# The seven-product output projection: weight sums by accumulating DMA, sums of y on VectorE with other signs, first product added to x2 from PSUM

## The chip, the cores and the metric

The kernel runs on one NeuronCore of a Trainium2 chip. The metric is device time in microseconds (us) of one execution. TensorE (PE in the profile, its weight loads PEld) multiplies, VectorE (DVE), ScalarE (ACT) and GpSimd (POOL) do the elementwise work, and SyncE (SP) issues nearly all transfers. Each engine takes its own instructions in order and waits on semaphores. [...]

## The reference, cut to what matters

One decoder block on 1024 tokens of width 1024, all in float32:

```
h  = RMSNorm(x)
p  = h @ w_in          -> q, k, v of two attentions, gate_swa, gate_mla
A  = sliding-window attention, B = latent attention
y  = sigmoid(gate_swa) * (A @ w_o_swa) + sigmoid(gate_mla) * (B @ w_o_mla)
x2 = x + y @ w_out                                  # the stage that is changed
out = RMSNorm(x2 + SwiGLU(RMSNorm(x2)))
```

## The kernel before

**Arithmetic.** A float32 product is made of three matmuls on numbers that are split into a high part (ScalarE, line 160, rounds it) and a low part (VectorE, line 161, subtracts). So every operand of a matmul costs one ScalarE pass and one VectorE pass. The tiles of the high and low parts of y are named yh and yl, those of w_out woh and wol.

**Seven products.** `y @ w_out` is done by Strassen's method in Winograd's form: y and w_out are cut into four blocks each, and seven block products, numbered 1, 2, 6, 7, 5, 4, 3 in the order in which they run (`X_ORDER`), replace eight. Three of them take sums of blocks of y, and four take sums of blocks of w_out. Each product has four row tiles t, each of 12 matmuls into one PSUM bank (tile xo). Products 1, 2, 5 and 3 use one set of four banks ("A"), products 6, 7 and 4 the other ("B"). Product 2 is added onto product 1 in the same banks, 7 onto 6, 4 onto 7, and 3 onto 5.

**Mixing steps.** Ahead of it, twelve steps (`steps`, a4, b0, b4, a5, ...) make the eight row strips of y. A step "a" multiplies by w_o_swa, a step "b" by w_o_mla. `mix_b` lets GpSimd multiply a strip by its gate (line 1304), then VectorE does a multiply from PSUM (line 1309) and an add (line 1310), and `y_split` makes the first high and low parts. After strips 4 to 7, `y_sums` makes four sums of y blocks on GpSimd, into two tiles ys and back into y. Between the steps `W_LOAD` and `W_WORK` load the four blocks of w_out (tiles wo), split two of them and make four sums of two halves each on GpSimd (`w_sum`; one goes to a tile wt).

**The product loop.** For each product and row tile it runs the 12 matmuls and then `xo_done`: product 1 is copied to SBUF by ScalarE (line 1570, tile xp), all others are added to the residual rows x2 by VectorE (line 175, `x<-xo,x`), and the copy of product 1 is added to x2 by GpSimd, twelve adds (`x<-xp,x`). A list `prep` of 30 splits for products 6, 7, 5, 4 and 3 is worked off between the row tiles, at a rate of 1.9 per tile from product 2 on. At (5, 3) GpSimd makes the first sums of the feed-forward weights (`ffn.mix(0)`, six passes, tiles sm and wr).

**Into the feed-forward network.** From product 4 on, each finished row block of x2 goes through `row_sum` (ScalarE square and sum, line 1583; GpSimd rstd, lines 295 and 298), `row_norm` (VectorE, line 1588, tile xn) and `to_h`, which transposes it on TensorE (line 1422, tile tp) and splits it. `next_h` calls `to_h`, first after product 4's tile t = 2. `Seven.run` runs one product of the feed-forward network; its first product is copied out of PSUM by ScalarE (line 793, tile pu).

**What sets the order.** From product 4 on, the order on TensorE, VectorE, ScalarE and GpSimd is that of the program text. Ahead of that a scheduler places the instructions, and buffers of two pools (21 small and 17 large) decide when a load can start. There, too, each engine runs strictly in the order that came out.

Of the kernel before, what the change touches and what calls it, by code (L numbers as in the profile page):

```python
# [12 lines left out]
ALU = mybir.AluOpType  # L13
# [76 lines left out]
def hybrid_block_kernel(  # L90
# [603 lines left out]
    class Seven:  # L694
# [623 lines left out]
    def y_split(q, k):  # L1318

        if k == 0:  # L1320
            yl[q] = (V("yh", F32R), V("yl", F32R))
        hi, lo = yl[q]
        src = {1: lambda: y[k][:, half(1)], 2: lambda: y[4 + k][:, half(1)], 6: lambda: y[k][:, half(0)],
               7: lambda: y_new[1][:, k], 5: lambda: y_new[0][:, k], 4: lambda: y[4 + k][:, half(0)],
               3: lambda: y[k][:, half(1)]}[q]()
        split(hi[:, k], lo[:, k], src)
        if q == 4:
            y.pop(4 + k)
        if q == 3:
            y.pop(k)  # L1330

    def y_sums(k):

        if k == 0:
            y_new.extend([V("ys") for _ in range(2)])
        s1, s3 = y_new[0][:, k], y_new[1][:, k]
# [6 lines left out]
    wr, wl, t1s = {}, {}, {}  # L1343

    def w_load(i, d):
        wr[(i, d)] = V("wo")
        nc.sync.dma_start(wr[(i, d)], w_out[i, d])

    def w_split(q, j):
# [4 lines left out]
        key = {1: (0, 0), 2: (1, 0), 6: (0, 0), 7: (0, 1), 5: None, 4: (1, 0), 3: (1, 1)}[q]  # L1354
        hi, lo = wl[q]
        split(hi[:, k], lo[:, k], t1s[j] if q == 5 else wr[key][:, k])

    def w_sum(n, j):
        k = slice(2 * j, 2 * j + 2)
        if n == 1:  # L1360
            t1s[j] = U("wt", F32, (P, 2, 512))
        b11, b12, b21, b22 = (wr.get((i, d)) for i in range(2) for d in range(2))
        b11, b12, b21, b22 = (None if w is None else w[:, k] for w in (b11, b12, b21, b22))
        sub(*{1: (t1s[j], b12, b11), 3: (b12, b22, b12), 2: (b11, b22, t1s[j]), 4: (b21, b21, b11)}[n], nc.gpsimd)
# [25 lines left out]
    split_ob(3, 1)  # L1390
    for k, (what, dc) in enumerate(steps):
# [11 lines left out]
        if k in W_LOAD:  # L1403
            w_load(*W_LOAD[k])
        for f, q in W_WORK.get(k, ()):
            for j in range(2):
                f(q, j)
# [3 lines left out]
    x2 = {}  # L1411
# [3 lines left out]
    def to_h(xn, b):  # L1415

        c = b % 4
        pss = []
        for kh in range(2):
# [3 lines left out]
            pss.append(ps)  # L1423
        if b < 4:
# [13 lines left out]
        t23 = U("t23", F32, (P, 2, 4, P))  # L1438
        sub(r[:, 0], pss[0], r[:, 0], nc.vector)
        nc.scalar.copy(t23[:, 1], pss[0])  # L1440
# [118 lines left out]
    p1o = V("xp1")  # L1559
# [4 lines left out]
    def residual(b, d, src, eng):  # L1564
        add(x2[b][:, half(d)], src, x2[b][:, half(d)], eng)
# [307 lines left out]
```

## Time and profile before

| what | value |
|---|---|
| median of 3 runs | 1367.27 us (1367.10 to 1368.41) |
| the profiled execution | 1367.46 us, of which 1365.7 us is the span of the trace |
| TensorE busy in the span | 1331.8 us (98%), 6552 matmuls |
| VectorE, ScalarE, GpSimd busy | 954.9 us, 652.0 us, 657.6 us |
| mean granted clock of TensorE | 0.996 of full speed |
| the product loop | 628.7 to 718.5 us from the span's start |

The profile's tables give, for a group or a single instruction, its start, its duration, and in brackets how long its engine sat idle before it and what released it. A busy time of TensorE counts matmuls that overlap, so what counts for the time are the stretches in which it is idle or in which its granted clock is below 1.

### The profile page before, as it was taken

The page shows a single profiled execution, that of the slowest core. Times are in us where ns is not written, and L with a number is a line of the kernel's source. Part 1 is how long each engine was busy: PE and PEld are TensorE (multiplying, and loading weights), DVE is VectorE, ACT ScalarE, POOL GpSimd, SP SyncE. Part 2 cuts the span into 40 slices and gives each one's busy share as a digit, 9 for nine tenths or more (in the row PEclk, how much of TensorE's full clock was granted, in tenths as well). Part 3 has the DMA queues.
Part 4 walks back from the last instruction along what each step waited for, and adds up shares of the span by engine and source line. Part 5 has one row for each costly group of instructions (what it writes and reads, how often), then busy time and mean ns, then how long its engine had stood idle before and what let it go on. Part 6 is the DMA issues. An engine that isn't in the chain of part 4 may idle for free. (4 is left out here: it accounts for less than half of the span.)

```text
span 1365.7 us, 18965 instructions
## 1 busy us (share of the span) xinstructions
PE 1331.8 (98%) x6552; PEld 1112.6 (81%) x6552; DVE 954.9 (70%) x1499; ACT 652.0 (48%) x1317; POOL 657.6 (48%) x664
## 2 busy tenths in 40 slices
PE   9999999999999999999989899999999999999997
PEld 6899878878788888887867688888888888888886
DVE  7868767676777886579978966666656655664862
ACT  7434766675567776633447323223322322644453
POOL 1115645552166554177644875766655651022421
PEclk9999999999999999999999999999999999999999
DMA  9454322335100110655041344554344415996504
GB/s 365 153 187 158 122 87 81 112 117 181 51 1 13 43 47 17 259 188 185 31 154 50 136 160 156 224 193 162 143 158 162 173 74 184 376 383 250 170 8 147
DMA packets 76945, 200.16 MB, mean 147 GB/s; under 512 B 8625, under 2 KB 15281, under 8 KB 76337
## 3 DMA queue, kind: packets, MB, share of 16 engines
q1 hardware_dynamic: 76704, 198.94, 41.0%
q8 instruction: 52, 0.85, 0.3%
q14 instruction: 45, 0.36, 0.1%
q10 hardware_dynamic: 144, 0.00, 0.0%
HBM read 139.14 MB, written 59.77 MB: 146 GB/s over the span
## 5 line engine op out<-in xcount | busy, mean ns | idle before, releaser
L161 DVE TENSOR_TENSOR wl<-wr,wl 128x512 fp32r<-128x512 f32 x150 | 156.4, 1064 | 76.6 <-ACT wl L160 76.3
L161 DVE TENSOR_TENSOR lrv<-lr,lrv 128x1024 fp32r<-128x1024 f32 x77 | 104.9, 1396 | 50.9 <-ACT lrv L160 47.2
L160 ACT CAST lrv<-lr 128x1024 fp32r<-128x1024 f32 x77 | 80.1, 1052 | 96.7 <-PE fd L169 55.7
L167 PE MATMUL fd<-lrv 128*128 128x512 f32 x308 | 119.8, 389 | 0.0
L168 PE MATMUL fd<-lrv 128*128 128x512 f32 x308 | 119.8, 389 | 0.0
L169 PE MATMUL fd<-lrv 128*128 128x512 f32 x308 | 119.8, 389 | 0.0
L172 POOL TENSOR_TENSOR wr<-wr,sm 128x512 f32<-128x512 f32 (+1 forms) x38 | 46.9, 1244 | 117.7 <-DVE wl L161 111.6
L160 ACT CAST wl<-wr 128x512 fp32r<-128x512 f32 x150 | 87.2, 622 | 3.3 <-DVE wr L816 2.7
L161 DVE TENSOR_TENSOR wl<-sm,wl 128x512 fp32r<-128x512 f32 x60 | 53.4, 915 | 45.5 <-ACT wl L160 45.5
L1146 POOL TENSOR_TENSOR denb<-denb,neg_one 128x1 f32<-128x1 f32 x64 | 36.5, 571 | 74.9 <-ACT p L1145 64.3
L167 PEld LDWEIGHTS fd<-lrv 128*128 128x128 f32 x308 | 57.8, 188 | 12.1
L168 PEld LDWEIGHTS fd<-lrv 128*128 128x128 f32 x308 | 57.8, 188 | 12.0
L169 PEld LDWEIGHTS fd<-lrv 128*128 128x128 f32 x308 | 57.8, 188 | 11.9
L1145 ACT ACTIVATE p<-scb,nmb 128x384 f32<-128x384 f32 (+3 forms) x64 | 47.6, 744 | 36.7 <-DVE nmb L1144 35.0
L161 DVE TENSOR_TENSOR ptl<-pTb,pth 128x512 fp32r<-128x512 f32 (+2 forms) x96 | 50.0, 549 | 13.7 <-ACT pth L160 12.8
L1144 DVE CUSTOM_DVE_ANT_0 scb<-scb,mask 128x384 f32<-128x384 f32 (+3 forms) x64 | 48.5, 757 | 14.0 <-PE scb L1136 13.7
L1478 ACT ACTIVATE act<-sm 128x512 f32<-128x512 f32 x11 | 7.0, 633 | 103.7 <-DVE sm L175 103.7
L295 POOL TENSOR_SCALAR ms<-ss 128x1 f32<-128x1 f32 x32 | 8.6, 270 | 98.6 <-ACT x L397 37.7
L1147 POOL TENSOR_SCALAR p<-p,denb 128x384 f32<-128x384 f32 (+3 forms) x64 | 49.3, 770 | 6.3
L175 POOL TENSOR_TENSOR du<-du,xq 128x512 f32<-128x512 f32 x8 | 16.3, 2054 | 69.5 <-DMA lr<-in_w_down_dram 50.4
L1478 ACT ACTIVATE act<-pu 128x512 f32<-128x512 f32 x22 | 13.9, 632 | 74.7 <-DVE pu L175 74.7
L160 ACT CAST pth<-pTb 128x512 fp32r<-128x512 f32 (+2 forms) x96 | 43.0, 482 | 13.5 <-PE pTb L1161 13.1
(355 smaller groups left out, 4475.1 us busy)
## 6 DMA issues: line engine op xcount, KB each, us to landing
lr<-la_d SPq DMA_DIRECT2D x77, 256.0 KB, 5.4
wr<-in_w_gate_dram SPq DMA_DIRECT2D x22, 512.0 KB, 4.3
wr<-in_w_up_dram SPq DMA_DIRECT2D x22, 512.0 KB, 5.0
wd<-in_w_down_dram SPq DMA_DIRECT2D x22, 512.0 KB, 6.7
rb_d<-wd SPq DMA_DIRECT2D x22, 512.0 KB, 2.6
la_d<-sd SPq DMA_DIRECT2D x22, 512.0 KB, 5.2
lr<-rb_d SPq DMA_DIRECT2D x44, 256.0 KB, 5.4
lr<-in_w_down_dram SPq DMA_DIRECT2D x33, 256.0 KB, 5.5
```

The source lines that it names most:

```text
L160: nc.scalar.copy(hi, src)
L161: (eng or nc.vector).tensor_tensor(lo, src, hi.bitcast(F32), op=ALU.subtract)
L167: nc.tensor.matmul(ps, ah, bh, start=first and i == 0, stop=False, skip_group_check=go_on)
L168: nc.tensor.matmul(ps, ah, bl, start=False, stop=False, skip_group_check=go_on)
L169: nc.tensor.matmul(ps, al, bh, start=False, stop=last and i == n - 1, skip_group_check=go_on)
L172: eng.tensor_tensor(out, a, b, op=ALU.subtract)
L175: eng.tensor_tensor(out, a, b, op=ALU.add)
L1144: nc.vector.tensor_tensor_reduce(s_, s_, m_, 1.0, -NEG, op0=ALU.add, op1=ALU.min, accum_out=nm)
L1145: nc.scalar.activation(p_, s_, AF.Exp, scale=-1.0, bias=nm, accum_out=den)
L1146: nc.gpsimd.tensor_tensor(den, den, neg_one[:, 0:1], op=ALU.pow)
L1147: nc.gpsimd.tensor_scalar(p[:, 0:w], p[:, 0:w], den, 0.0, op0=ALU.mult, op1=ALU.add)
L1478: nc.scalar.activation(dst, src, AF.Silu)
```

## The change

**Weights.** `w_sum` is gone. Each sum of w_out blocks is now made by a DMA that adds its source to what stands in its destination (`w_acc`, issued by GpSimd, in two halves). Blocks are loaded as before through SP; the block (0, 0) is loaded twice, once as the start of the sum t1. Where a difference is needed, ScalarE turns the sign of a block in place first (`w_neg`). Two of the operands come out with the wrong sign, and their split turns it: ScalarE casts with scale -1, VectorE uses one `scalar_tensor_tensor` (lines 1363 and 1364 of the changed kernel) in place of the subtract. The loads and sums start at step 1, where before the first load was at step 4.

**y.** The four sums are formed on VectorE, with signs turned so that one of the two ys tiles falls away.

**First product.** It is no longer copied by ScalarE. VectorE adds or subtracts it from its PSUM bank to three halves of x2 for each t, twelve adds in place of four copies and GpSimd's twelve adds. All eight x2 loads come earlier in the program, at steps 10 and 11.

**Order.** The prep list starts in product 1. `ffn.mix(0)` is cut in two and stands behind the second and fourth `row_sum`. `next_h` can run a product between the transposes and the work on them, which is used once, and the copy `t23[:, 1]` stands ahead of the subtract.

```diff
-        def mix(self, j, eng=None):
+        def mix(self, j, eng=None, m=None):
-            if (j, self.ms[0]) in self.sums:
-                return
-            for m in self.ms:
+            for m in self.ms if m is None else (m,):
+                if (j, m) in self.sums:
+                    continue
...
     def y_sums(k):
-            y_new.extend([V("ys") for _ in range(2)])
+            y_new.append(V("ys"))
...
-        add(s1, a21, a22, nc.gpsimd)
-        sub(s3, a11, a21, nc.gpsimd)
-        sub(a21, s1, a11, nc.gpsimd)
-        sub(a11, a12, a21, nc.gpsimd)
+        add(s1, a21, a22, nc.vector)
+        add(a21, a11, a21, nc.vector)
+        add(a11, s1, a11, nc.vector)
+        add(a12, a11, a12, nc.vector)
...
+    def w_neg(name):
+        for j in range(2):
+            w = wr[name][:, 2 * j:2 * j + 2]
+            nc.scalar.activation(w, w, AF.Copy, scale=-1.0)
+
+    def w_acc(name, src):
+        for j in range(2):
+            k = slice(2 * j, 2 * j + 2)
+            src_ = wr[src][:, k] if isinstance(src, str) else w_out[src[0], src[1]][:, k]
+            nc.gpsimd.dma_start(wr[name][:, k], src_, accum_op=ALU.add)
...
-    W_LOAD = {4: (0, 0), 5: (0, 1), 6: (1, 1), 8: (1, 0)}
-    W_WORK = {7: [(w_split, 1)], 9: [(w_sum, 1)], 10: [(w_sum, 3)], 11: [(w_split, 2), (w_sum, 2)]}
+    W_WORK = {1: [(w_load, "b12", 0, 1)], 2: [(w_load, "t1", 0, 0)], 3: [(w_neg, "b12"), (w_acc, "t1", "b12")],
+              4: [(w_load, "b11", 0, 0)], 5: [(w_acc, "b12", (1, 1))], 6: [(w_split, 1, 0)],
+              7: [(w_split, 1, 1), (w_load, "b21", 1, 0)], 8: [(w_acc, "b11", "b12")], 9: [(w_split, 2, 0)],
+              10: [(w_split, 2, 1)], 11: [(w_neg, "b21"), (w_acc, "b21", "b11")]}
...
     def xo_done(q, t):
-        if q == 1:
-            nc.scalar.copy(p1o[:, t], ps)
-        else:
-            residual(*{2: (4 + t, 0), 6: (4 + t, 1), 7: (t, 1), 5: (t, 1), 4: (t, 0), 3: (4 + t, 1)}[q], ps, nc.vector)
-        if q in (6, 7):
-            residual({6: 4, 7: 0}[q] + t, 1, p1o[:, t], nc.gpsimd)
-        if q == 7:
-            residual(t, 0, p1o[:, t], nc.gpsimd)
+        for b, d, sign in {1: ((t, 0, 0), (t, 1, 0), (4 + t, 1, 1)), 2: ((4 + t, 0, 1),), 6: ((4 + t, 1, 0),), 7: ((t, 1, 1),),
+                           5: ((t, 1, 0),), 4: ((t, 0, 1),), 3: ((4 + t, 1, 1),)}[q]:
+            x_ = x2[b][:, half(d)]
+            (add if sign else sub)(x_, x_, ps, nc.vector)
...
+            if (q, t) == (6, 0):
+                w_load("b22", 1, 1)
-            if (q, t) == (5, 3):
-                ffn.mix(0)
-            n_x += q != 1
-            while prep and 30 - len(prep) < 1.9 * n_x:
+            n_x += 0.4 if q == 1 else 1.8
+            while prep and 30 - len(prep) < n_x:
+                if r + t in (1, 3):
+                    ffn.mix(0, None, "gu"[r + t == 3])
...
-    next_h()
-    ffn.run()
+    next_h(ffn.run)
```

The order that comes out moves rows at these places. Names carry the buffer's number.

**GpSimd between step b1 and the product loop.** Before, with the last gate products (L1304) among sums of y (ys, sg) and of w_out (wt, wo):

```order
L1304 TENSOR_TENSOR sg_6713<-ar_6364,sg_6713 128x1024
L172 TENSOR_TENSOR ys_6632<-sg_6590 128x512
L175 TENSOR_TENSOR ys_6631<-sg_6590,sg_6552 128x512
L172 TENSOR_TENSOR sg_6590<-ys_6631,sg_6590 128x512
L172 TENSOR_TENSOR sg_6590<-sg_6552,sg_6590 128x512
L1304 TENSOR_TENSOR sg_6842<-ar_6448,sg_6842 128x1024
L172 TENSOR_TENSOR wt_6923<-wo_6760,wo_6711 128x1024
L172 TENSOR_TENSOR wt_6925<-wo_6760,wo_6711 128x1024
L172 TENSOR_TENSOR wo_6760<-wo_6798,wo_6760 128x1024 x2
```

Now, from the gate product of step b1 to the first rstd (ms, rstd):

```order
L1304 TENSOR_TENSOR sg_6592<-ar_6195,sg_6592 128x1024
L1352 DMA wo_6638<-wo_6590 128x1024 x2
L1352 DMA wo_6590<-in_w_out_dram 128x1024 x2
L1304 TENSOR_TENSOR sg_6720<-ar_6364,sg_6720 128x1024
L1304 TENSOR_TENSOR sg_6849<-ar_6448,sg_6849 128x1024
L1352 DMA wo_6718<-wo_6590 128x1024 x2
L1352 DMA wo_6847<-wo_6718 128x1024 x2
L295 TENSOR_SCALAR ms_7416<-ss_7414 128x1
L298 TENSOR_TENSOR rstd_7418<-ms_7416,neg_half 128x1
```

GpSimd has no elementwise pass left between the last gate product and the first rstd; four pairs of accumulating DMAs stand there, two pairs of them ahead of the gate product of step b2.

**GpSimd at the rstd of the first four row blocks.** Behind the second rstd now stand three passes of the feed-forward sums, and then the third rstd:

```order
L295 TENSOR_SCALAR ms_7439<-ss_7437 128x1
L298 TENSOR_TENSOR rstd_7441<-ms_7439,neg_half 128x1
L175 TENSOR_TENSOR sm_7445<-wr_7324,wr_7349 128x512
L172 TENSOR_TENSOR sm_7445<-sm_7445,wr_7324 128x512
L172 TENSOR_TENSOR wr_7324<-wr_7324 128x4x128
L295 TENSOR_SCALAR ms_7468<-ss_7466 128x1
L298 TENSOR_TENSOR rstd_7470<-ms_7468,neg_half 128x1
```

Before, the six passes stood ahead of the first rstd, and the eight rstd followed each other with one pass between the last two.

**ScalarE after the third transposed block of the second half.** Before, the copy of the transposed block (t) and its cast stood ahead of the copy of a finished product (pu):

```order
L1440 COPY t_1454_7805<-tp_7795 128x512
L1442 CAST t2h_7677<-t_1454_7805 128x4x128
L793 COPY pu_7824<-fa_7811 128x512
L1448 CAST b22h_7675<-tp_7800 128x4x128
L1449 CAST t3h_7679<-t_1454_7805 128x4x128
```

Now the copy of the product stands first:

```order
L793 COPY pu_7816<-fa_7803 128x512
L1446 COPY t_1453_7818<-tp_7793 128x512
L1449 CAST t2h_7675<-t_1453_7818 128x4x128
L1455 CAST b22h_7673<-tp_7798 128x4x128
L1456 CAST t3h_7677<-t_1453_7818 128x4x128
```

TensorE's own order is the same in both kernels.

More of the change, by code (lines that the diff above doesn't have):

```diff
@@ L1402, in hybrid_block_kernel, with to_ps @@
         st.conv_to(weights_of(k + 1))
[L1403 to L1407, printed above, removed]
+        for f, *args in W_WORK.get(k, ()):
+            f(*args)
+        if k >= 10:
+            for b in {10: (4, 0, 5, 1), 11: (6, 2, 7, 3)}[k]:
+                x2[b] = load_x(b)
     raw1 = {}
-    x2 = {}
     late = []
     hq.clear()
-    def to_h(xn, b):
-        c = b % 4
+    def to_ps(xn):
         pss = []
@@ L1590, in row_norm, with next_h @@
         xns.append((xn, b))
-    def next_h():
+    def next_h(mid=None):
         xn, b = xns.pop(0)
-        r = to_h(xn, b)
+        pss = to_ps(xn)
+        if mid is not None:
+            mid()
+        r = to_h(pss, b)
         if r is not None:
```

50 lines of the change are left out of this document (18 added, 32 removed).

## The prediction

> **What bounds the kernel now.** I read the page's busy times first, then TensorE's list of waits around the stage that is changed (540 to 900 us), then the windows of that stretch, then the instructions in order of time.
>
> ```profile
> PE 1331.8 (98%) x6552; PEld 1112.6 (81%) x6552; DVE 954.9 (70%) x1499; ACT 652.0 (48%) x1317; POOL 657.6 (48%) x664
> ```
>
> TensorE bounds the kernel, and its matmuls stay the same in number and order. So the change can only win or lose where TensorE waits or runs at a lower clock. These are its waits there:
>
> ```profile
> PE tp L1422 <- DVE xn L1588: 5.6, 1, 5.6
> PE fa L169 <- DVE wl L161: 2.6, 1, 2.6
> PE fb L169 <- DVE wl L161: 1.7, 2, 1.3
> PE fa L167 <- ACT pu L793: 1.6, 1, 1.6
> PE xo L169 <- DVE yl L161: 1.0, 1, 1.0
> ```
>
> The first is the transposes of the first row block, which wait for VectorE's normalized rows; the last is product 1, which waits for a low part of y. Both lie in the changed stage. The windows (PE, PEld, DVE, ACT, POOL busy, then the granted clock) show what the first brings with it:
>
> ```profile
> 690.00:700.00 10.00, 4.39 (x21) 3.54 (x20) 7.65 (x9) 3.31 (x6) 6.21 (x7) 0.85 0.26 105
> 700.00:710.00 10.00, 10.00 (x43) 8.22 (x42) 6.75 (x10) 6.08 (x11) 1.48 (x4) 0.81 0.83 265
> ```
>
> The clock sinks to 0.85 and 0.81, as in no other window from 540 to 900. The instructions around it, PE, DVE, ACT, POOL, DVE, PE:
>
> ```profile
> 692.59 0.39 PE L169 MATMUL xo<-woh,yl 128*128 128x512 f32 x1
> ...
> 693.60 0.68 DVE L175 TENSOR_TENSOR x<-xo,x 128x512 f32<-128x512 f32 x1
> ...
> 694.36 1.06 ACT L1583 ACTIVATE xn<-x 128x1024 f32<-128x1024 f32 x1 [17.05 <-issue]
> ...
> 695.88 0.55 POOL L298 TENSOR_TENSOR rstd<-ms,neg_half 128x1 f32<-128x1 f32 x1
> ...
> 697.26 1.27 DVE L1588 SCALAR_TENSOR_TENSOR xn<-x,rstd,ffng 128x1024 f32<-128x1024 f32 x1
> ...
> 698.59 1.97 PE L1422 MATMUL tp<-ident,xn 128*128 128x128 f32 x8 [5.61 <-DVE xn L1588]
> ```
>
> Product 4's tile t = 2 ends at 692.98. A tile is 12 matmuls; by the row of 628.90:683.30 below (53.38 us for 236) one starts every 0.227 us, 2.72 us a tile; so t = 0 ended at 687.5. VectorE adds it to x2 only at 693.60: it is **6.1 us late**, and this lateness, not the chain behind it, makes the wait. From that add to the transposes are 4.99 us, while TensorE has 5.44 us of work (t = 1 and 2) to cover them.
>
> Why VectorE is late:
>
> ```profile
> 628.90:683.30 54.40, 53.38 (x236) 43.84 (x235) 52.59 (x47) 24.81 (x38) 36.61 (x20) 1.00 0.18 59
> ...
> 649.00:655.50 6.50, 6.50 (x31) 5.37 (x30) 6.21 (x9) 3.85 (x6) 0.00 (x0) 1.00 0.00 0
> ...
> 650.41 1.21 DVE L161 TENSOR_TENSOR wol<-wo,woh 128x1024 fp32r<-128x1024 f32 x1
> 651.54 0.68 DVE L161 TENSOR_TENSOR yl<-sg,yh 128x512 fp32r<-128x512 f32 x1
> ...
> L161 DVE TENSOR_TENSOR yl<-sg,yh 128x512 fp32r<-128x512 f32 x14 | 19.8, 1425 | 1.6 <-ACT yh L160 1.6
> L161 DVE TENSOR_TENSOR wol<-wo,woh 128x1024 fp32r<-128x1024 f32 x10 | 19.3, 1933 | 0.0
> L161 DVE TENSOR_TENSOR yl<-ys,yh 128x512 fp32r<-128x512 f32 x8 | 9.7, 1228 | 0.0
> L161 DVE TENSOR_TENSOR wol<-wt,woh 128x1024 fp32r<-128x1024 f32 x2 | 3.5, 1760 | 0.0
> L175 DVE TENSOR_TENSOR x<-xo,x 128x512 f32<-128x512 f32 x17 | 11.6, 679 | 1.1 <-PE xo L169 1.1
> ```
>
> In the product loop VectorE is busy 52.59 of 54.40 us. In the 6.5 us in which GpSimd does nothing, a 128x512 split takes 0.68 and a 128x1024 split 1.21 us; over 628 to 694 us (the five groups) they average 1.23 to 1.43 and 1.76 to 1.93. The adds from PSUM take 0.68 throughout. So splits with both inputs in SBUF are stretched by GpSimd's passes, adds from PSUM are not.
>
> **The change part by part.**
>
> *GpSimd's passes go.* Between the last gate product and the first rstd it has none. The 22 splits of yl and 12 of wol in those groups take 52.3 us; at the quiet durations 22 x 0.68 + 12 x 1.21 = 29.5. That frees 22.8 us.
>
> *VectorE's new work.* Twelve adds of product 1, read from PSUM, take 0.68 us each: 8.2 us. Of the 16 sums of y the last four fall into the loop, each like a quiet split: 4 x 0.68 = 2.7. The twelve others fall into the mixing steps, 8.2 us in 60, where VectorE's stretched passes shrink too. The `scalar_tensor_tensor` splits have a near row in L1588 (1.27 against 1.21): four of them, 0.2 us. Sum 11.1, against 22.8 freed. VectorE then has some 41 us of work in those 54, and an add follows its matmuls at once. Unknown is only whether the stretching goes wholly: if the rest is between 0 and 22.8 us, the end is anywhere from no lateness to 11.1 us more; I take it at nothing, since the quiet 6.5 us show the bare durations on the same tiles.
>
> *First wait.* With the add on time, the transposes can start 4.99 us after t = 0, under the 5.44 that cover them: 5.61 us go.
>
> *The clock.*
>
> ```profile
> 704.04 0.40 PE L167 MATMUL xo<-woh,yh 128*128 128x512 f32 x1
> ...
> 707.46 1.03 PE L1422 MATMUL tp<-ident,xn 128*128 128x128 f32 x8
> ...
> 710.41 0.39 PE L167 MATMUL xo<-woh,yh 128*128 128x512 f32 x1
> ```
>
> From the transposes at 698.59 to the tenth matmul behind them at 704.04 are 5.45 us; the same stretch a tile later, 707.46 to 710.41, takes 2.95. So 2.50 us go with the wait.
>
> [...]
>
> *Wait for yl in product 1.* It was VectorE late in the mixing steps, with the same cause: 1.02 us go. Between these steps TensorE waited for nothing, and VectorE's 8.2 us of sums are covered by what GpSimd's sums stretched there. One point is new: the second operand's split stands in VectorE's order ahead of the last strips, behind the load of block (1, 0).
>
> ```profile
> 621.39 0.38 SPq L1347 DMA_DIRECT2D wo<-in_w_out_dram  x1
> ...
> 628.00 1.05 ACT L160 CAST woh<-wo 128x1024 fp32r<-128x1024 f32 x1 [7.53 <-DMA wo<-in_w_out_dram]
> ```
>
> It needs a large buffer that step a7 reads. The steps are 24 matmuls, 5.44 us each, and end at 628.9, so a7, the third from the end, runs from 612.6 to 618; I estimate that the load leaves near 615.5, 6 us sooner. Should it land at 628.0 as before, up to 2 us come back.
>
> *Moved feed-forward sums.*
>
> ```profile
> 683.52 1.74 POOL L175 TENSOR_TENSOR sm<-wr,wr 128x512 f32<-128x512 f32 x1
> 685.34 2.16 POOL L172 TENSOR_TENSOR sm<-sm,wr 128x512 f32<-128x512 f32 x1
> 687.46 1.74 POOL L172 TENSOR_TENSOR wr<-wr 128x512 f32<-128x512 f32 x1
> ```
>
> Three passes, 5.64 us, now stand ahead of the third rstd. Counted from the end of t = 2: the second rstd ends at +0.3 (2.83 us after its add), the passes at +5.9, the third rstd at +6.8, VectorE's rows at +8.1. TensorE wants them after three more tiles and two sets of transposes (0.79 each by the start of the next matmul): +9.7. Nothing is lost, with 1.6 us to spare. But VectorE, in order, stands still for that rstd and the adds queue behind it; I estimate that its work on the rows is then 1.1 us later against TensorE when the feed-forward network begins. Bounds 0 and 3.
>
> *The pu copy.*
>
> ```profile
> 738.09 0.59 ACT L1440 COPY t<-tp 128x512 f32<-128x512 f32 x1 [2.73 <-DVE hraw L172]
> ...
> 739.41 0.58 ACT L793 COPY pu<-fa 128x512 f32<-128x512 f32 x1
> ...
> 760.00:780.00 20.00, 17.39 (x77) 14.06 (x76) 17.74 (x18) 5.41 (x10) 17.28 (x11) 1.00 0.21 79
> ```
>
> ScalarE stood 2.73 us for VectorE with that copy queued behind, and TensorE waited 1.6 for it. Now the copy stands first: 1.58 go, if VectorE's load behind doesn't take them back. The waits for wl (2.6 and 1.7) stay.
>
> *Accumulating DMAs.* No row shows one. What waits: GpSimd issues the second pair when the first has landed, and the gate product of step b2 stands behind both.
>
> ```profile
> 605.45 0.70 DVE L1310 TENSOR_TENSOR sg<-sg,sg 128x512 f32<-128x512 f32 x1
> ...
> wo<-in_w_out_dram SPq DMA_DIRECT2D x4, 1024.0 KB, 8.1
> ...
> rb_d<-wd SPq DMA_DIRECT2D x22, 512.0 KB, 2.6
> ...
> 580.17 2.95 ACT L1217 ACTIVATE sg<-sg 128x1024 f32<-128x1024 f32 x3
> ```
>
> ScalarE turns the sign in place of those sigmoids, some 2.1 us from 580.2; VectorE wants the gate product (2.4 us) at 605.45. That leaves 20.7 us for two rounds, 10.4 each. Bounds of a round, which moves 1 MB: 2.6 and twice 8.1; nearest is the 1 MB load, 8.1, so nothing is lost. At 16.2 GpSimd would be 11.6 us late, and VectorE with it, against about 11 us of PSUM banks and its air in the loop: 0 to 3 us.
>
> **Sum.** 5.61 + 2.50 + 1.02 + 1.58 - 1.1 = 9.6 us. The profiled execution took 1367.46 (span 1365.7 and 1.8 around it), 0.2 above the median of the runs: **1357.9 us**, 0.7% less.
>
> **The rivals.**
>
> *VectorE becomes the bound* (slower). If the splits stay slow without GpSimd, the 11.1 us of new work come on top of a queue with 1.8 us of air: the add of product 4 comes 9.3 us later still, and so does the loop's end, about 1376. It decides as soon as less than 11.1 of the 22.8 us are freed. For it: 97% busy now. Against it: the quiet stretch. 0.07.
>
> *The accumulating DMAs hold GpSimd's queue.* VectorE stops at step b2, and the four banks of products there fill; slower than before if a round takes over 20 us, 2.5 times the nearest row. About 1370. 0.05.
>
> [...]
>
> *The gain is cut short.* The moved sums run over their 1.6 us, or the load of block (1, 0) is late: a wait of 2 to 5 us returns at the transposes or at product 2. About 1362. For it: both margins are 1 to 3 us. 0.15.
>
> *All waits of the stretch go*, also those for wl, if VectorE enters the network with no queue: 4.3 us more, 1353. Against it: VectorE is busy 17.74 of 20 us at 760 to 780, with passes that stay. 0.08.
>
> *No effect*, because the wait only moves to later row blocks: 1366. 0.04.
>
> **How the numbers follow.** The forecast (1356 to 1360.5) has 0.61. The range of 1352.5 to 1364.5 takes it in, with most of the case cut short and most of the case in which all waits go: about 0.8. A difference of 0.2%, 2.7 us, is about what a measurement of this kernel can tell from none. Faster: 0.61 + 0.08 and three quarters of 0.15, 0.80. Within 0.2%: the rest of that and the case without effect, 0.08. Slower: 0.12.
>
> **What would show it.** Right: no wait of the transposes for xn, no window with a clock under 1 between 680 and 720, splits at 0.68 and 1.21 us in the loop, the add of product 4's t = 0 within 1 us of its last matmul, the loop's end at about 709 instead of 718.5. Wrong: VectorE over 95% busy in the loop, TensorE waiting for wol or woh of product 2 or 6, a wait of VectorE for GpSimd's rstd over 3 us, or GpSimd idle over 20 us ahead of the gate product of step b2.

## The result, and the profile after

| | median | runs | ratio to before, 95% interval |
|---|---|---|---|
| before, beside it | 1367.84 us | 4, 1367.10 to 1369.05 | |
| changed | 1359.99 us | 4, 1358.32 to 1360.56 | 0.9940 (0.9923 to 0.9957) |
| changed, measured again (e9 below) | 1362.73 us | 5, 1362.19 to 1363.67 | 0.9966 (0.9953 to 0.9978) |

The change makes the kernel faster, by 7.9 us in the first measurement and by 4.6 in the second. Both lie in the range of 1352.5 to 1364.5, the second outside the forecast of 1356 to 1360.5; why one kernel gave two times is one of the things that the experiments had to find. The profiled execution of the first took 1360.19 us, 7.27 less than the one before.

TensorE's waits from 540 to 900 us in the changed kernel (waiting operation, what it waited for: us in total, times, longest):

```profile
PE fa L169 <- DVE wl L161: 2.6, 1, 2.6
PE fb L169 <- DVE wl L161: 1.6, 2, 1.2
PE fa L167 <- ACT pu L793: 1.1, 1, 1.1
PE fb L168 <- DVE t2l L172: 0.8, 1, 0.8
PE fb L167 <- DVE pu L175: 0.2, 1, 0.2
```

The wait of the transposes for xn and the wait of product 1 for yl are gone. All that is left lies in the feed-forward network: 6.3 us, where it was 6.4. The product loop in the changed kernel, as a window (PE, PEld, DVE, ACT, POOL busy, then the granted clock) and by groups (busy, mean ns of one):

```profile
628.90:683.30 54.40, 54.40 (x241) 45.06 (x240) 45.57 (x67) 22.19 (x32) 1.72 (x2) 1.00 0.33 98
```

```profile
L161 DVE TENSOR_TENSOR yl<-sg,yh 128x512 fp32r<-128x512 f32 x17 | 11.5, 686 | 0.7 <-ACT yh L160 0.7
...
L161 DVE TENSOR_TENSOR wol<-wo,woh 128x1024 fp32r<-128x1024 f32 x7 | 8.5, 1217 | 0.0
L1364 DVE SCALAR_TENSOR_TENSOR wol<-wo,woh 128x1024 fp32r<-128x1024 f32 x4 | 4.9, 1219 | 0.0
```

VectorE is busy 45.57 us of 54.40 instead of 52.59, although it has the adds of product 1 as well, and all splits take their bare time of 0.69 and 1.22 us. Around the end of product 4's first two tiles, in order of time:

```profile
687.38 0.69 DVE L175 TENSOR_TENSOR x<-x,xo 128x512 f32<-128x512 f32 x1 [1.43 <-PE xo L169]
...
689.62 0.56 POOL L298 TENSOR_TENSOR rstd<-ms,neg_half 128x1 f32<-128x1 f32 x1
...
691.00 1.28 DVE L1587 SCALAR_TENSOR_TENSOR xn<-x,rstd,ffng 128x1024 f32<-128x1024 f32 x1
...
692.62 1.03 PE L1424 MATMUL tp<-ident,xn 128*128 128x128 f32 x8
```

Now VectorE waits for TensorE at the add, not the other way round. To place the gain I cut each profiled execution at three rows: the first gate load of the stage (SP, `sg<-gate_d`), the first transpose of xn (PE, tile tp), and the first matmul of product 5 of the feed-forward network (PE, `fa<-t1h`). From their starts:

| | to the first gate load | A: to the first transpose | B: to product 5 | C: to the end | span |
|---|---|---|---|---|---|
| before | 558.92 | 139.67 | 60.76 | 606.35 | 1365.7 |
| changed | 560.04 | 132.58 | 58.92 | 606.86 | 1358.4 |
| difference | +1.12 | -7.09 | -1.84 | +0.51 | -7.3 |
| forecast | 0 | -6.63 | -2.98 | 0 | -9.6 |

The forecast has its first wait and yl in A, the clock, the pu copy and the moved sums in B. So A came out as told and a little better. Missing are 1.1 us in B, and 1.6 us in stretches whose instructions the change leaves as they were.

### The profile page after: what moved, and what is told of

The parts are those of the page before. It is cut to its first block, busy times and chain, and to the rows that moved or that the text cites. A ratio compares the mean times of both kernels' runs of the same rounds, so it can differ in the third digit from the quotient of the medians.

```text
span 1358.4 us, 18967 instructions
## 1 busy us (share of the span) xinstructions
PE 1331.8 (98%) x6552; PEld 1112.0 (82%) x6552; DVE 944.6 (70%) x1527; ACT 653.4 (48%) x1317; POOL 596.2 (44%) x636
## 4 chain that ended last, share of the span: by engine, by line
PE 72%; DVE 7%; ACT 4%; issue 3%; POOL 3%; DMA 0%; POOLq 0%; ACTq 0%; DVEq 0%
PE fa L169 7%; PE fa L167 7%; PE fa L168 7%; PE fd L168 5%; PE fd L167 5%; PE fd L169 5%; PE fb L167 5%; PE fb L169 5%; PE fb L168 5%; DVE wl L161 2%; PE pTb L1161 2%; PE xo L167 1%; PE xo L168 1%; PE xo L169 1%; PE oA L167 1%
## 5 line engine op out<-in xcount | busy, mean ns | idle before, releaser
L169 PE MATMUL fa<-t1h,wl 128*128 128x512 f32 x120 | 46.8, 391 | 2.6 <-DVE wl L161 2.6
```

Source lines behind the costliest of these rows:

```text
L169: nc.tensor.matmul(ps, al, bh, start=False, stop=last and i == n - 1, skip_group_check=go_on)
```

## The experiments

Theory A, from the prediction: VectorE was late because GpSimd's passes stretch its splits. Rival B: VectorE simply had too many passes, or got them too late. The table has all twelve runs, cut at the same rows; "wl" is the wait of TensorE for VectorE's split of the next step's weights in the mixing steps, and the clocks are those granted in the 10 us around that place and in the 8.5 us from 2.5 us after the start of product 5.

| run | median, us | ratio (95%) | A | B | C | wl | clocks |
|---|---|---|---|---|---|---|---|
| e1 before, no adds | 1358.48 | 0.9939 (0.9923 to 0.9956) | 133.88 | 58.24 | 606.30 | - | 1.00, 1.00 |
| e2 product 1 by copy | 1362.28 | 0.9955 (0.9938 to 0.9972) | 135.09 | 58.97 | 607.47 | 2.2 | 1.00, 0.80 |
| e3 GpSimd, two inputs | 1361.51 | 0.9960 (0.9942 to 0.9977) | 136.48 | 58.97 | 606.42 | 2.1 | 0.83, 1.00 |
| e4 GpSimd, one input | 1358.81 | 0.9937 (0.9920 to 0.9954) | 132.82 | 59.05 | 607.46 | - | 1.00, 0.80 |
| e5 pu undone | 1362.08 | 0.9955 (0.9941 to 0.9970) | 134.83 | 58.92 | 607.79 | 1.9 | 1.00, 0.80 |
| e6 sums undone | 1362.86 | 0.9957 (0.9942 to 0.9972) | 136.70 | 58.28 | 607.90 | 2.2 | 0.83, 0.80 |
| e7 second sums early | 1361.19 | 0.9949 (0.9934 to 0.9964) | 132.57 | 63.24 | 604.44 | - | 1.00, 1.00 |
| e8 gate on VectorE | 1358.60 | 0.9928 (0.9912 to 0.9945) | 132.83 | 58.97 | 607.83 | - | 1.00, 0.80 |
| e9 changed again | 1362.73 | 0.9966 (0.9953 to 0.9978) | 136.78 | 58.96 | 607.72 | 2.3 | 0.83, 0.80 |
| e10 gate and sums | 1360.90 | 0.9954 (0.9942 to 0.9966) | 132.87 | 63.34 | 604.34 | - | 1.00, 1.00 |
| e11 y sums on GpSimd | 1359.18 | 0.9940 (0.9926 to 0.9953) | 132.58 | 58.95 | 607.52 | - | 1.00, 0.80 |
| e12 w sums on GpSimd | 1367.06 | 0.9995 (0.9986 to 1.0004) | 140.29 | 58.96 | 607.70 | - | 1.00, 0.80 |

### e1: take GpSimd's adds away, and nothing else

```diff
-        if q in (6, 7):
-            residual({6: 4, 7: 0}[q] + t, 1, p1o[:, t], nc.gpsimd)
-        if q == 7:
-            residual(t, 0, p1o[:, t], nc.gpsimd)
```

This kernel leaves out what these adds give to x2.

> The kernel before without GpSimd's twelve adds of product 1 onto x2 (that part of x2 is left out). VectorE's and TensorE's instructions stay the same, instruction for instruction. Theory A (VectorE is late because GpSimd's passes stretch its splits): from about 656 us on the splits take 0.68 and 1.21 us instead of 1.2 to 1.9, the add of product 4's t = 0 comes within 1 us of its matmuls, and the wait of the transposes for xn (5.6 us) and the half clock behind it (2.5 us) go: about 8 us less than before, 1359 to 1361; the 1.0 us wait of product 1 for yl stays. Rival B (VectorE has too many passes in the loop, or gets them too late, and GpSimd has no part in it): no change, 1366 to 1368.

TensorE's waits of this kernel, 540 to 900 us:

```profile
PE fa L169 <- DVE wl L161: 2.6, 1, 2.6
PE fb L169 <- DVE wl L161: 1.7, 2, 1.3
PE fa L167 <- ACT pu L793: 1.6, 1, 1.6
PE xo L169 <- DVE yl L161: 1.0, 1, 1.0
...
```

This is the list of the kernel before, row for row, without its first row. The two largest groups of VectorE's splits, 628 to 694 us:

```profile
L161 DVE TENSOR_TENSOR wol<-wo,woh 128x1024 fp32r<-128x1024 f32 x10 | 17.8, 1783 | 0.0
L161 DVE TENSOR_TENSOR yl<-sg,yh 128x512 fp32r<-128x512 f32 x14 | 15.7, 1131 | 2.3 <-ACT yh L160 2.3
```

No instruction of VectorE was taken away, its 34 splits take 41.2 us in place of 52.3, and the wait that VectorE caused is gone: theory A holds, and rival B falls. It was not a wait for GpSimd's adds either, since in the kernel before VectorE waited in this stretch only for ScalarE (1.6 us) and TensorE (1.1). From 648 us on every split takes the expected 0.68 or 1.21 us to 0.01, apart from the five between 670 and 680, beside the six passes of `ffn.mix(0)` at 668.65 to 679.40. Column B of the table is 2.52 us shorter, the half clock. The 1.0 us for yl stayed, as expected, and is worth 1.30 us in A (133.88 against 132.58).

### e2, e3, e4: put GpSimd's passes back into the changed kernel

e2 has product 1's copy on ScalarE and its twelve adds on GpSimd as before. e3 and e4 add passes that nothing reads (band is a tile that is free by then):

```diff
         split(hi[:, k], lo[:, k], src)
+        for n in range(2 * (q not in (1, 2))):
+            c = slice(256 * n, 256 * n + 256)
+            sub(band, src[:, c], hi[:, k, c].bitcast(F32), nc.gpsimd)     # e3
+            nc.gpsimd.tensor_copy(band, src[:, c])                        # e4, in its place
```

> The changed kernel with product 1 as before: ScalarE's copy and GpSimd's twelve adds, no adds of VectorE from PSUM. In the kernel before 36.6 us of GpSimd passes in the loop went with 22.8 us of stretching, 0.62 us per us. Theory A: twelve adds of some 1.8 us are 22 us of GpSimd, 14 us of stretching, against 8.2 us of adds that VectorE no longer makes: its work in the loop is about 51 of 54.4 us, it is late again by 2 to 5 us, and the transposes wait 0 to 4 us: 1360 to 1366. Rival B (GpSimd has no part in it): VectorE has 8.2 us less to do, no wait comes back, 1359 to 1361, and the splits stay at 0.68 and 1.21 us.

> The changed kernel, and GpSimd forms the low part of each of the 20 y splits of the loop a second time into a scratch tile, in 40 passes of 128x256 with both inputs in SBUF that nothing reads: some 26 to 36 us of GpSimd in the loop, nothing more for any other engine. Theory A: 16 to 22 us of stretching, VectorE's work in the loop rises from 45.6 to over 60 us, more than its 54.4: the wait of the transposes comes back with 5 us or more and the half clock with it, 1366 to 1374. Rival B (GpSimd has no part in it): 1359 to 1361.

> As the run before it, but GpSimd's 40 passes are copies with one input in SBUF instead of subtracts with two. Theory A1 (what stretches VectorE's splits is any pass of GpSimd over SBUF): splits stretched as in the run before it, per us of GpSimd, and some us slower than the changed kernel. Theory A2 (only a pass with two inputs takes the place that a split needs): splits at 0.68 and 1.21 us, no wait, 1359 to 1361. I hold A1 for somewhat likelier, with less stretching.

The groups of e3 between 628 and 694 us:

```profile
L172 POOL TENSOR_TENSOR band<-sg,yh 128x256 f32<-128x256 f32 x32 | 35.6, 1113 | 3.2 <-ACT yh L160 0.9
L161 DVE TENSOR_TENSOR yl<-sg,yh 128x512 fp32r<-128x512 f32 x18 | 15.3, 860 | 0.9 <-ACT yh L160 0.9
L161 DVE TENSOR_TENSOR wol<-wo,woh 128x1024 fp32r<-128x1024 f32 x8 | 11.0, 1381 | 0.8 <-ACT woh L160 0.8
```

and of e4:

```profile
L1327 POOL COPY band<-sg 128x256 f32<-128x256 f32 x26 | 16.3, 627 | 3.4 <-DVE sg L175 1.9
L161 DVE TENSOR_TENSOR yl<-sg,yh 128x512 fp32r<-128x512 f32 x17 | 12.4, 737 | 0.7 <-ACT yh L160 0.7
L161 DVE TENSOR_TENSOR wol<-wo,woh 128x1024 fp32r<-128x1024 f32 x6 | 7.4, 1229 | 0.0
```

The same window of the loop, PE, PEld, DVE, ACT and POOL busy, in the changed kernel

```profile
628.90:690.00 61.10, 61.10 (x271) 50.60 (x270) 48.82 (x71) 23.85 (x35) 2.29 (x4) 1.00 0.31 95
```

and in e3:

```profile
628.90:690.00 61.10, 61.10 (x271) 50.62 (x270) 57.23 (x71) 22.78 (x33) 47.02 (x42) 1.00 0.32 102
```

The direction of theory A holds: splits are stretched by subtracts with two inputs (0.86 and 1.38 us) and hardly by copies with one (0.74 and 1.23), so of the two readings of e4 the second, A2, is nearer, not the one that I held likelier. Per us of GpSimd, too, e4 cost less: 20.4 us more of it gave VectorE 1.0 us more, 0.05 per us. But the copies are also shorter (0.40 us at least, the subtracts 0.74), so these runs do not tell the number of inputs from the length. The size of theory A does not hold. In e3 GpSimd does 44.7 us more, and VectorE's work rises by 8.4 us, 0.19 us per us of GpSimd instead of 0.62, and still fits into the 61.1. The first transpose comes 62.56 us after the first matmul of product 1 in the changed kernel and in e2, e3 and e4 alike: no wait came back in the loop. In e2 VectorE is busy 43.41 of the 54.40 us where theory A gave 51, with splits of yl of 0.90 us. A rate taken over one stretch is no constant of the two engines: 0.62 in the loop of the kernel before, 0.19 in e3, 0.05 in e4.

What e2 and e3 lost they lost ahead of the loop, in a wait for wl that none of their edits touches. That is the next question.

### e9 and e8: why the same kernel gives two times

e9 is the changed kernel once more. e8 moves one pass:

```diff
-            nc.gpsimd.tensor_tensor(ga, ar.pop(dc), ga, op=ALU.mult)
+            (nc.vector if dc == 3 else nc.gpsimd).tensor_tensor(ga, ar.pop(dc), ga, op=ALU.mult)
```

> The changed kernel itself again, on the same chip as the three runs beside it. Theory U (a matter of tenths of a us decides whether GpSimd's gate product of step b3 or VectorE's split of wl comes first): of its runs some are near 1358 and some 2 to 4 us above; in those that are profiled the stage takes 132.6 us from the first gate loads to the first transposes, or 135 to 136.5 with a wait of TensorE for wl of about 2 us. Theory V (the wait belongs to the edits of e2, e3, e5 and e6): 132.6 us, all runs within 1.5 us.

> The changed kernel with the gate product of step b3 on VectorE instead of GpSimd. In the two runs e2 and e3 that product ran on GpSimd at 601.6 and 600.6 us, behind the accumulating DMAs, at the same time as VectorE's split of wl, which then took 3.40 and 3.39 us instead of 1.2, and TensorE waited 2.2 and 2.1 us in step b2's successor (in the changed kernel's profile the split came 0.6 us ahead of it and took 1.21). Theory U (it is a matter of tenths of a us which comes first, so some executions of the changed kernel pay 2.2 to 4 us): no such wait here, 132.6 us from the stage's first gate loads to the first transposes, all timed runs within 1.5 us of one another, median 1357 to 1359. Theory V (the wait of e2 and e3 belongs to their own edits): same time and spread as the changed kernel, 1358.3 to 1360.6.

VectorE and GpSimd in the mixing steps, in order of time, first in the changed kernel's first profile:

```profile
597.37 0.68 DVE L161 TENSOR_TENSOR yl<-sg,yh 128x512 fp32r<-128x512 f32 x1
597.44 0.89 POOL L1352 DMA_DIRECT2D wo<-in_w_out_dram  x1 [3.02 <-DMA wo<-wo]
...
598.00 2.77 POOL L1304 TENSOR_TENSOR sg<-ar,sg 128x1024 f32<-128x1024 f32 x1
598.69 2.64 DVE L1310 TENSOR_TENSOR sg<-sg,sg 128x512 f32<-128x512 f32 x1
601.25 1.21 DVE L161 TENSOR_TENSOR wl<-wr,wh 128x1024 fp32r<-128x1024 f32 x1
601.86 2.85 POOL L1304 TENSOR_TENSOR sg<-ar,sg 128x1024 f32<-128x1024 f32 x1 [1.09 <-ACT sg L1217]
```

and in e9, with the matmul that waits:

```profile
595.39 0.89 POOL L1352 DMA_DIRECT2D wo<-in_w_out_dram  x1 [2.40 <-ACT yh L160]
595.57 3.71 DVE L161 TENSOR_TENSOR yl<-sg,yh 128x512 fp32r<-128x512 f32 x1
595.95 2.77 POOL L1304 TENSOR_TENSOR sg<-ar,sg 128x1024 f32<-128x1024 f32 x1
...
600.05 2.77 POOL L1304 TENSOR_TENSOR sg<-ar,sg 128x1024 f32<-128x1024 f32 x1 [1.33 <-ACT sg L1217]
600.52 3.39 DVE L161 TENSOR_TENSOR wl<-wr,wh 128x1024 fp32r<-128x1024 f32 x1
...
603.97 0.51 PE L169 MATMUL oB<-obT,wl 128*128 128x512 f32 x1 [2.30 <-DVE wl L161]
```

In these rows the two engines take turns. In e9 the gate product runs to 598.72 us, and the split of yl, 0.68 us of work, ends at 599.28; the next gate product runs to 602.82, and the split of wl ends at 603.91. In the first profile the same split of yl is over at 598.05, when the gate product begins, and the split of wl starts 0.6 us ahead of the second one. e9 began the stage 1.80 us earlier (558.24 against 560.04); corrected for that, its gate product of b2 started 0.25 us sooner than in the first profile, and its second gate product at the same time to 0.01 us. So in these two profiles a quarter of a microsecond decides. In the first profile the gate products held back VectorE too, but passes for which TensorE did not wait: an add (2.64 us) and a sum of y (2.88). What sets the start of the first gate product is the row ahead of it: the issue of the second pair of accumulating DMAs, which waited for the first pair. (For e9 the profile names a ScalarE cast; by the trace the first pair had landed 0.35 us ahead of the issue, as in the first profile.) Before the change the gate product of b2 stood here, that of b3 at 603.20, and TensorE had no wait:

```profile
588.00 2.40 POOL L1304 TENSOR_TENSOR sg<-ar,sg 128x1024 f32<-128x1024 f32 x1
```

The wait costs A 2.3 to 2.5 us (e2, e5) or 3.9 to 4.2 (e3, e6, e9), where the clock sinks to 0.83 behind it. Of the seven profiled runs that leave this place as the change made it (the first, e2, e3, e5, e6, e7, e9), five have it; in e4 four of the copies stand here too and move the gate product of b3 to 605.64. e8, with the second gate product on VectorE behind the split of wl, has no such wait, A is 132.83, and its median is 1358.60. Theory U holds, except that the runs of e8 still spread over 3.4 us (1357.72 to 1361.12) instead of 1.5, and that all five of e9 lie above 1362 rather than some. e8 has the lowest ratio of all runs; its interval lies clear of that of e9, though not of the first measurement's.

### e5 and e6: the two terms at the network's start

e5 puts the transposes and the copy back where they were; e6 puts the six passes of `ffn.mix(0)` back at (5, 3):

```diff
-    next_h(ffn.run)                                  # e5
+    next_h()
+    ffn.run()
...
-        nc.scalar.copy(t23[:, 1], pss[0])            # e5
         sub(r[:, 0], pss[0], r[:, 0], nc.vector)
+        nc.scalar.copy(t23[:, 1], pss[0])
...
-                if r + t in (1, 3):                  # e6
-                    ffn.mix(0, None, "gu"[r + t == 3])
+            if (q, t) == (5, 3):
+                ffn.mix(0)
```

> The changed kernel with the transposes and the copy t23[:, 1] at product 2 of the network as before (next_h and then the product, the copy behind VectorE's subtract). In the changed kernel it is 58.9 us from the first transposes to the first matmul with t1 (product 5 of the network). Theory P (as predicted: the order of the copy is worth 1.58 us): 60.4 us there, the wait for pu 2.6 us, 1.5 us slower in all. Theory Q (VectorE is the bound in that stretch, 18.2 of 20 us, and takes back what the copy gains): 58.4 to 59.4 us, the wait for pu about 1.6 and the one for t2l about 0.3 us, no change of the whole.

> The changed kernel with the six passes of the first feed-forward sums back at (5, 3), ahead of product 4. GpSimd has nothing else to do there, so they start when their weights have landed, about 640 us, and run in 10 to 13 us beside splits with 15 us of air in the loop. Theory P (as predicted: the sums behind the second and fourth row sum cost 1.1 us at the network's start): VectorE no longer waits 1.35 us for the third rstd, 57.8 us from the first transposes to product 5 of the network instead of 58.9, 1.1 us faster in all. Theory Q (that place costs nothing, since VectorE has air until product 1 of the network): 58.6 to 59.2 us, no change. Theory R (the loop has no air for them): the wait for xn comes back, 2 us slower or more.

e5, TensorE's waits between 700 and 760 us:

```profile
PE fa L167 <- ACT pu L793: 2.1, 1, 2.1
...
PE fb L168 <- DVE t2l L172: 0.3, 1, 0.3
```

B is 58.92, with and without the edit. Undone, the wait for pu grows by 1.0 and the one for t2l shrinks by 0.5; the matmuls of tile fb start 0.56 us later (45.18 against 44.62 us after the first transpose), and product 5 still starts at the same time. Theory Q holds: ScalarE's place in the queue was worth nothing here, where VectorE is the one that all wait for. In e6 GpSimd began the sums in the loop, behind a split of yl:

```profile
653.28 1.27 POOL L175 TENSOR_TENSOR sm<-wr,wr 128x512 f32<-128x512 f32 x1 [18.82 <-DVE yl L161]
```

No wait came back in the loop; B is 58.28. The place that the change gave these sums costs 0.64 us, between P (1.1) and Q (none). Both runs have the wait for wl in A, so their medians tell of that and not of these edits.

### e7 and e10: the sums that stretch the network's splits

The 2.6 us left at wl look like the same mechanism: `ffn.mix(1)` runs on GpSimd at 750 to 761 us. e7 makes these passes behind the sixth and eighth row sum. e10 has e8's and e6's edits and makes them behind the fourth and sixth.

> The changed kernel with GpSimd's six passes of the second pair of feed-forward sums, which run at 750 to 761 us beside VectorE's splits of wl (2.84 and 3.47 us for two), moved ahead: three behind the sixth row sum, three behind the eighth. Theory S (the wait of 2.6 us for wl is the same stretching again): the splits of wl at 750 to 758 us take 0.7 to 1.2 us each, the waits of 2.6 and 1.2 us shrink by 2 to 4 us together, 55 to 57 us from the first transposes to product 5 instead of 58.9. Theory T (VectorE has too many passes there, quiet or not, or the passes only stretch others at 709 to 735 us): 58.5 to 60 us.

> The changed kernel with three moves that e6 to e8 point to: the gate product of step b3 on VectorE (no wait for wl in the mixing steps), the first feed-forward sums back at (5, 3) (0.6 us less up to product 5 of the network), and the second sums behind the fourth and the sixth row sum instead of at 750 us (the splits of wl at 754 us less stretched: the wait of 2.6 us falls to about 1). Theory S (all of this is GpSimd's passes in VectorE's way): 132.6 us to the first transposes, about 58.3 from there to product 5, 604.5 to 605.5 behind it; 1356 to 1357.5 us, 1.5 to 4 below the changed kernel. Theory T (the passes stretch other splits as much where they are now, as the early second sums of e7 did): 1358 to 1360 us.

GpSimd and VectorE of e7 where the second half of the passes went, and TensorE behind it:

```profile
718.26 2.13 POOL L172 TENSOR_TENSOR sm<-sm,wr 128x512 f32<-128x512 f32 x1
```

```profile
719.19 3.46 DVE L161 TENSOR_TENSOR wl<-wr,wl 128x512 fp32r<-128x512 f32 x2
```

```profile
736.70 0.50 PE L167 MATMUL fa<-b21h,wl 128*128 128x512 f32 x1 [3.39 <-ACT pu L793]
...
756.56 0.50 PE L169 MATMUL fa<-t1h,wl 128*128 128x512 f32 x1 [0.85 <-DVE wl L161]
```

Both theories have a part of it. The wait for wl falls from 2.6 to 0.85 us, and C by 1.9 to 2.4 us against the kernels with a clock of 1.00 there, so it was GpSimd in VectorE's way. But two splits at 719 us that took 1.29 us together now take 3.46, the chain behind them is late, and B grows by 4.3. From the first transpose to the end e7 is 1.9 us slower than the changed kernel (667.68 against 665.78). e10 found no free place either: its passes waited 2.47 us for their weights and held an rstd behind them, and TensorE waited 1.7 us for b11l; 667.68 again. No version of mine beat e8.

### e11 and e12: which sums had to leave GpSimd

e11 gives the 16 sums of y back to GpSimd. e12 replaces the accumulating DMAs from tile to tile:

```diff
+            if isinstance(src, str):
+                add(wr[name][:, k], wr[name][:, k], wr[src][:, k], nc.gpsimd)
+                continue
```

> The changed kernel with the 16 sums of y on GpSimd instead of VectorE, signs and places as they are. VectorE has 11 us less to do, GpSimd some 23 us more, 16 of them in the mixing steps. Theory W (VectorE's splits and GpSimd's passes take turns, so a split that meets a pass waits for its end): the splits of wl and y in the mixing steps are stretched by up to a pass, product 1 waits for yl again by about 1 us, 133.5 to 135 us from the first gate loads to the first transposes instead of 132.6; 0 to 3 us slower. Theory X (the sums cost the same on either engine, since VectorE has air): 132.6 us, no change.

> The changed kernel with three of its four accumulating DMAs (those from tile to tile) made by GpSimd adds of 128x1024, six passes of some 2.6 us; the one from w_out in DRAM stays. Theory Y (the DMAs are what keeps these sums off the engines): the adds meet VectorE's last splits at 619 to 636 us, each of which then waits up to 2.6 us; TensorE waits for yl or wol of products 1 and 2, 1 to 4 us from the first gate loads to the first transposes more than 132.6. Theory Z (before the loop there is air enough, and the DMAs only hold GpSimd's queue ahead of the gate products): 132.6 us, and no wait for wl in the mixing steps, since the gate product of step b2 is done by 592 us instead of 600.8.

e12, GpSimd at the end of the mixing steps, two adds of VectorE in the same time, the first add of product 1, and TensorE:

```profile
630.72 6.18 POOL L175 TENSOR_TENSOR wo<-wo,wo 128x1024 f32<-128x1024 f32 x2 [6.23 <-ACT wo L1346]
```

```profile
631.74 2.90 DVE L1310 TENSOR_TENSOR sg<-sg,sg 128x512 f32<-128x512 f32 x1
...
635.28 2.17 DVE L1310 TENSOR_TENSOR sg<-sg,sg 128x512 f32<-128x512 f32 x1
...
641.53 0.68 DVE L172 TENSOR_TENSOR x<-x,xo 128x512 f32<-128x512 f32 x1
```

```profile
644.66 0.80 PE L167 MATMUL xo<-woh,yh 128*128 128x512 f32 x1 [4.47 <-DVE x L175]
```

e11 is no slower (A 132.58): theory X, and W falls, at least for this run, which also escaped the wait for wl. Of e12, theory Y holds in its direction, by another wait than it named. Product 2 accumulates into the banks of product 1, so it can't start before VectorE has read product 1's first tile three times; with VectorE late behind two GpSimd passes of 3.1 us, TensorE stands still for 4.47 us and then runs at a lower clock (0.70 on average from 640 to 650 us), A is 7.7 us longer, and the whole gain of the change is gone (0.9995). So with the order of this kernel it is the accumulating DMAs that make product 1's adds on VectorE affordable; another place for GpSimd's sums was not tried. In the kernel before, where ScalarE emptied product 1's banks, GpSimd's sums of w_out alone did no such harm: e1 has them and lost only the 1.0 us for yl.

## Why the prediction was right or wrong

**Right: what bounded the kernel, the first wait, the clock.** The add of product 4's t = 0 comes with its matmuls (687.38, 6.2 us earlier than before), the transposes wait for nothing, the clock is 1.00 in the loop, and the splits have the bare durations that the quiet 6.5 us had shown. e1 shows the cause with a kernel in which only GpSimd's adds are missing: the first wait was worth 5.79 us in A against 5.61 forecast, the clock 2.52 in B against 2.50.

**Right in size, cause not isolated: yl.** This wait is gone and was worth 1.30 us against 1.02. Which part of the change took it away is not shown: e11 has the y sums on GpSimd again, e12 most sums of w_out, and neither waits for yl. The load of block (1, 0), put at 615.5 us, left at 616.65 in a stage that began 1.12 later, and the cast behind it came at 624.07 instead of 628.00.

**Mis-sized, without cost: "some 41 us of work in those 54".** Measured were 45.57. The 22.8 us freed were counted over 628 to 694 us and taken off a row of 54.40 us. Inside that row the kernel before has 19 splits of yl and 10 of wol, 44.2 us in place of 25.0 at the quiet durations. That frees 19.2 and gives 44.5.

**Wrong in size: the pu copy.** The step "Now the copy stands first: 1.58 go" gave 0.00 us (e5). The prediction had named the condition, VectorE's load behind it, and quoted the row for it (17.74 of 20 us), but still booked the full term.

**Wrong in size: the moved sums.** Booked with -1.1, measured -0.64 (e6). VectorE waits 1.35 us for the third rstd and catches up on a part. Pu and sums together were forecast at +0.48 and came to -0.64; that is the 1.1 us missing in B.

**Wrong: "Accumulating DMAs ... nothing is lost".** The prediction allowed two rounds of 10.4 us ahead of the gate product of b2. Only one stands there, since the product waits for the second pair to be issued and not for its landing (GpSimd in the changed kernel; 597.44 above is the issue of the second half):

```profile
583.27 1.99 POOL L1352 DMA_DIRECT2D wo<-wo  x2 [4.47 <-ACT wo L1346]
593.55 0.86 POOL L1352 DMA_DIRECT2D wo<-in_w_out_dram  x1 [8.29 <-DMA wo<-wo]
```

This round took 14.2 us to that issue, more than 10.4, and the gate product was still done by 600.8, long before VectorE's add with it (line 1310) at 609.09. The step failed because it asked only when the gate product must be ready. It is also a pass of 2.8 us that shuts VectorE's splits out while it runs, and the DMAs moved it by 9 us (598.00 against 588.00, with a start 1.12 later) onto the splits of yl and wl. In the first profile that cost TensorE nothing; in five of seven profiles it cost 2.3 to 4.2 us in A. This is the rival of the DMAs that hold GpSimd's queue, in a smaller form than its 20 us a round: the queue was held, and what suffered was another engine's pass. The profiled run of e9, which has the second time of 1362.73, shows this cost with 4.2 us. That the first measurement fell into 1356 to 1360.5 was in part luck.

**Not put to the test: the point from which rivals decide.** "VectorE becomes the bound" was to decide "as soon as less than 11.1 of the 22.8 us are freed". e3 gave VectorE 8.4 us of it back, so that some 14 were still freed, and nothing was late. That agrees with the point and does not reach it.

**Not the change's.** The start (+1.12) and C (+0.51) differ from one execution to the next: over the fourteen profiles the first gate load lies between 557.68 and 560.04 us, behind instructions that are the same in all of them. In the eleven profiles other than e7, e10 and the first, C falls into two groups: 606.30 to 606.42 with the clock at 1.00 and 607.46 to 607.90 with 0.80 behind the wait for wl. The first, at 606.86 and a clock of 1.00, lies between them; its TensorE rows from product 5 on take as long as those of e3, to 0.04 us, and the 0.5 us lie behind the last matmul (7.57 us to the end of the span against 7.13 in e3 and 7.06 before).

**Open.** Whether the earlier start of the split list in product 1 or the earlier loads of x2 matter by themselves was not tried. Why the five timed runs of e9 all took over 1362 us while the four of the first measurement did not, I can't say: only profiled runs show the wait.

## What to carry to other kernels

In these traces a pass with two SBUF inputs on GpSimd and one on VectorE took turns (in e9 a split of 1.22 us took 3.39 beside a gate product of 2.77), so a GpSimd pass is priced by what it meets on VectorE and who waits for that, not by its own deadline; moving it by a few us, here by a DMA ahead of it in its queue, can cost more than it takes (up to 4.2 us in A for that pass of 2.77). A wait that a reordering on ScalarE seemed to remove was worth nothing (B 58.92 with it and without, e5) while VectorE, which all of them wait for, had no air. A wait of TensorE is not priced by its length alone either: 2.2 us brought the clock to 0.83 in e6 and left it at 1.00 in e2. And one profile of a kernel may be the lucky one: where two engines meet within tenths of a microsecond, profile it more than once before pricing the rest.

## What the runs showed of the hardware

**Taking turns.** VectorE's split of 128x1024, 1.22 us, took 3.39 when it met a gate product of 2.77 us, and ended 1.09 us after it; a 128x512 split of 0.68 took 3.71 and ended 0.56 after it. With GpSimd passes of 128x256 both sides paid: GpSimd's took 1.11 us on average and 0.74 at least, VectorE's splits 0.86 instead of 0.69. GpSimd's copies with one input cost the splits 0.05 us and took 0.57 to 0.63 us on average, 0.40 at least.

Which of two passes holds the other is not shown. The split of wl in e9 began 0.47 us behind the gate product and was held. The split of yl there has its row 0.38 us ahead of the gate product's (595.57 against 595.95) and was held all the same, so the start of a row does not tell. GpSimd's copies, which read SBUF too, held VectorE little; whether for their one input or for their shorter time (0.40 us at least, the subtracts 0.74), these runs do not tell. GpSimd's eight accumulating DMA issues in the changed kernel took 0.85 to 1.21 us each.

**The clock sinks after short waits, by where they lie.** After waits of 1.9 to 2.3 us for wl in the mixing steps the clock fell in three of five profiles, after the wait of 2.6 us for wl in the network in eight of twelve, and it cost some 1 to 2 us each time (C 606.4 against 607.7, A 134.8 to 135.1 against 136.5 to 136.8). Equal waits did and did not bring it down (2.2 us in e6 and in e2), so it is not the length alone that decides.

The record of the granted clock in the traces tells them apart. Within a profile its changes lie whole multiples of 3.413 us from one another. In the kernel before the clock is full from 4.11 us on, at a half from 697.02, full again from 703.84 and at a half from 1362.61, behind the last matmul: 203, 2 and 193 such steps. In e6 it falls at 604.54 and at 758.14 us, 45 steps apart. So I divided each profile into windows of this length with the changes on their edges. The clock was halved behind the window in which TensorE was idle for all 3.41 us (before, 693.60 to 697.02) and behind the one with 2.23 (e6, 601.13 to 604.54). It stayed full behind those with 1.84 (before, 761.87 to 765.28, in the wait of 2.6 us for wl), 1.87 (e7) and 1.38 (e2). In e6 the wait of 2.2 us lies inside one window, in e2 an edge cuts it into 1.38 and 0.84 us, and in e7 the wait of 3.39 us for pu is cut into 1.87 and 1.52 and left the clock at 1.00. Two windows of each in this order (PE, PEld, DVE, ACT, POOL busy, then the clock):

```profile
601.13:604.54 3.41, 1.18 (x6) 0.67 (x5) 3.41 (x2) 0.44 (x1) 1.91 (x1) 1.00 1.03 326
604.54:607.96 3.42, 3.42 (x10) 2.68 (x9) 3.28 (x6) 0.61 (x1) 0.00 (x0) 0.50 0.86 298
...
601.17:604.58 3.41, 2.03 (x9) 1.33 (x8) 3.38 (x3) 0.33 (x1) 2.70 (x1) 1.00 1.04 277
604.58:607.99 3.41, 2.57 (x11) 2.16 (x12) 3.38 (x6) 1.06 (x1) 0.00 (x0) 1.00 0.89 281
...
731.76:735.18 3.42, 1.55 (x7) 0.94 (x5) 3.23 (x5) 1.23 (x3) 2.67 (x3) 1.00 0.20 77
735.18:738.59 3.41, 1.89 (x8) 1.59 (x9) 3.31 (x5) 1.96 (x4) 1.35 (x2) 1.00 0.00 0
```

So part of a window was enough to halve the clock, 2.23 of 3.41 us in e6, and 1.87 in e7 was not.
